# A hybrid decoder layer on one core: decode-state steps reordered, the second half of the up projection's operands put in another order, and the last quarter of the output finished like the other three

## Chip, cores and metric

The kernel runs on one core of one Trainium2 chip. The metric is the device time of one execution in microseconds (us). Each kernel is run several times and the median is given; the kernel before took 1743.32 us (three runs: 1743.06, 1743.32 and 1748.29).

## What is computed

One layer of a decoder, for a prompt of 1024 tokens and, beside it, 8 single new tokens of other sequences ("decode", with states given). All arrays are float32.

```python
D_MODEL, SEQ, DEC_BATCH, D_FF = 1024, 1024, 8, 2816
def decoder_layer(x, S_h, S_s, buf_s, buf_f, lb, w):
    h = rmsnorm(x, w['norm1_w'])
    q_r, f_r, i_r, g_r, z, xbc_r, dt_r = jnp.split(h @ w['w_in'], splits, axis=-1)
    ...
    o_a, S_h_new = hgrn2_mix(q, k, v, log_f, S_h)          # 8 heads, gated linear recurrence
    o_a = rmsnorm(o_a, w['hgrn_norm_w']) * silu(g_r)
    xbc, buf_s_new = causal_dwconv(xbc_r, buf_s, ...)
    ...
    y, S_s_new = ssd_scan(X * dt[..., None], A * dt, Bh, Ch, S_s)   # 16 heads, Mamba-2
    y = rmsnorm((y + D * X) * silu(z), w['ssm_norm_w'])
    x = x + concat([o_a, y]) @ w['w_out']
    h = rmsnorm(x, w['norm2_w'])
    gate, val = jnp.split(h @ w['w_up'], 2, axis=-1)       # 1024 -> 2 x 2816
    gate, buf_f_new = causal_dwconv(gate, buf_f, ...)      # width 3
    x = x + (silu(gate) * val) @ w['w_down']               # 2816 -> 1024
    return x, S_h_new, S_s_new, buf_s_new, buf_f_new
y = rmsnorm(x, final_norm_w)
```

The new states of both mixers and the last rows of both convolutions are outputs too. For a decode token the Mamba part is one step: the new state is `Sd = decay * Sd + B * x`, and its output is the sum over the state of `Sd * C`.

## The kernel before

**Precision.** Each large product runs as three TensorE (PE) products: both factors are split into a rounded part and a remainder (`hi` by a cast on ScalarE, ACT; `lo = x - hi` on VectorE, DVE), and high x high, high x low and low x high are summed. A group of products sums into one PSUM bank; some other engine then evicts the bank, and until it has done so no new group can start in that bank. There are three banks called `mm` for the big products (`ua` and `dn` below are such banks) and four called `mx` for all else (`ub`, `sT`, `st`, `yo`, `yd`, `fin`), and one `nx`.

**Stages**, by time in the profiled execution: input projection with both recurrences (to 805 us), output projection (to 1013), up projection (to 1466), down projection (to 1704), the final norm's blocks (to the end at 1741).

**What sets the order.** The order of the matmuls on PE is written out by hand: big products come as "jobs" that yield after every few matmuls, and small work is woven in between: `spread(x, n)` advances the generator `x` once in every n matmuls, `after(n, f)` calls `f` n matmuls later, `drive` and `finish` run jobs up to a named one. On the other engines and in the DMA queue (SP) a scheduler puts the instructions in an order from their data dependences and its own estimates; `tc.issue_after(i)` forbids it to place an instruction ahead of `i`. Each engine then works strictly in its order, so an instruction that waits holds up all that stand behind it there.

**The decode step of Mamba** (`ssm_decode`, lines 656 to 675) runs for 8 pairs of heads. For each and for four tokens at a time it loads `Bb` and `Cb` (B and C of the tokens, spread over the partitions) and `Sd` (the state); ACT multiplies `Sd` by the decay (line 669), DVE multiplies `Bb` by x (line 670) and adds it to `Sd` (671), GpSimd (POOL) multiplies by `Cb` (673), and DVE sums (674). This runs beside the last steps of the prompt's recurrence: `ssd_back` makes a chunk's output and the next state `S` (line 611), and `ssm_state_out` (633) transposes the final state on PE (bank `sT`, line 636), copies it on DVE to `so` (638) and stores it. The stage is called z here.

**The up projection.** For each of 22 column blocks j the product of a 2 x 2 block matrix of activations with a 2 x 2 block matrix of weights (gate and value columns) is made with seven products `p1` to `p7` in place of eight, Strassen's scheme in Winograd's form; it needs sums of blocks ahead of it and sums of products behind it. It is done for two rows of activation blocks, i = 0 (the first 516 tokens) and i = 1 (the other 516). `set_of(i)` prepares the seven operands: `comb` makes a sum `sm` (line 1352), `put` splits an operand into `uh` and `ul` (lines 1344 and 1345). `up_sums(j)` makes four sums of weights `wt` on POOL (line 1424); `up_split` splits these into `wh` and `wl` (1443, 1444). Of the products behind, `p7` adds on DVE (1478) and then has two subtractions on POOL (1479, 1480: `val` and `us`); `p2`, `p4` and `p3` add on DVE into `fext` (1486, 1494) and `val` (1506). For j = 0, row 0 comes whole before row 1 (order `FIRST`), and `set_of(1)` runs beside it. `set_norm(i, c)` makes the norm of a quarter of the tokens: one matmul into bank `n2ms` and three steps of DVE (lines 737 to 739, `nt`).

**The down projection** (`down`) sums 4 blocks of k at a time into a bank `dn` and adds it to x in DVE (line 1611). `act_load` splits its activations into `ah` and `al` (line 1154).

**The end.** The last two blocks of k are done by quarter of the tokens, in the order 3, 0, 1, 2. For quarters 3, 0 and 1: 48 `dn` matmuls, DVE adds them to x (line 1688), PE transposes x to rows of tokens (line 1695, bank `fin`), ACT squares and sums (1697), then a mean, a root, and the scaling: the first half of the columns in one DVE operation (1707), the second by an ACT copy (1704) and a POOL product; each half is stored. Quarter 2 is done in another way (`last_blocks`, lines 1655 to 1674): the product is made with tokens as rows at once, and x is added by multiplying it, split in two, with the identity on PE.

## Time and profile before

| | |
|---|---|
| median of three runs | 1743.32 us |
| the profiled execution's own time | 1742.79 us |
| its span, first to last instruction | 1741.1 us |
| PE, matmuls | 1705.4 us busy (98%) |
| PE, weight loads (beside the matmuls) | 1656.5 us (95%) |
| DVE | 1089.1 us (63%) |
| ACT | 789.8 us (45%) |
| POOL | 483.4 us (28%) |
| mean clock granted to PE | 0.997 of full speed |

The profiled execution is 1.7 us longer than its span, and half a microsecond under the median. "Busy" is the time in which at least one instruction of the engine ran; for PE the ends of matmuls are modelled. In rows of the timeline the first number is the start of an instruction in us from the start of the span, the second its duration; then engine, line of the code, operation, tile written `<-` tiles read, and in brackets the idle time of the engine just ahead of it with what ended this.

### The profile page before, as it was taken

What the parts mean: (1) busy time and instruction counts of PE and PEld (TensorE: products, weight loads), DVE (VectorE), ACT (ScalarE), POOL (GpSimd) and SP (SyncE); (2) the same over time, 40 slices, a digit from 0 to 9 for tenths busy, and PEclk for the clock granted to TensorE, in tenths of its full rate; (3) what the DMA queues carried; (4) which work ended last, traced back from release to release, by engine and by line L of the source; (5) the groups of instructions that cost most, each with busy time, mean ns of one, the idle gap of its engine ahead of it and who ended that gap; (6) DMA issues with size and microseconds to landing.
All of it is one profiled execution on the core that took longest, in us unless ns stands there. A gap on an engine that the chain in (4) does not pass through costs nothing. (4 is left out here: it accounts for less than half of the span.)

```text
span 1741.1 us, 38505 instructions
## 1 busy us (share of the span) xinstructions
PE 1705.4 (98%) x16111; PEld 1656.5 (95%) x16111; DVE 1089.1 (63%) x1983; ACT 789.8 (45%) x1441; POOL 483.4 (28%) x501
## 2 busy tenths in 40 slices
PE   7999999999999999999999989999999999999998
PEld 7999999999999999999999989999999999999997
DVE  6668666555565565567746777667676668544454
ACT  7677686344454354545334554333344334111124
POOL 2102131110120122011222266666666664000002
PEclk9999999999999999999999999999999999999999
DMA  5354334633434425335347712222222226322212
GB/s 165 73 123 120 96 91 144 186 103 105 130 94 120 115 88 142 118 99 178 119 145 252 230 53 87 97 74 74 74 80 80 97 75 240 138 90 77 86 44 98
DMA packets 250212, 200.22 MB, mean 115 GB/s; under 512 B 48020, under 2 KB 221574, under 8 KB 250022
## 3 DMA queue, kind: packets, MB, share of 16 engines
q1 hardware_dynamic: 249750, 197.67, 37.2%
q8 instruction: 126, 2.06, 0.5%
q14 instruction: 48, 0.39, 0.1%
q0 software_dynamic: 288, 0.10, 0.0%
HBM read 155.16 MB, written 46.95 MB: 116 GB/s over the span
## 5 line engine op out<-in xcount | busy, mean ns | idle before, releaser
L93 PE MATMUL mm<-hl,wh 128*128 128x344 f32 x1248 | 405.5, 325 | 0.0
L93 PE MATMUL mm<-hh,wh 128*128 128x344 f32 x1248 | 405.0, 325 | 0.0
L93 PE MATMUL mm<-hh,wl 128*128 128x344 f32 x1248 | 402.0, 322 | 0.0
L93 PEld LDWEIGHTS mm<-hl,wh 128*128 128x128 f32 x1248 | 235.4, 189 | 4.8 <-issue 4.2
L93 PEld LDWEIGHTS mm<-hh,wh 128*128 128x128 f32 x1248 | 235.4, 189 | 3.4 <-issue 2.8
L93 PEld LDWEIGHTS mm<-hh,wl 128*128 128x128 f32 x1248 | 235.6, 189 | 1.4 <-issue 1.2
L199 ACT CAST wh<-ws 128x1024 fp32r<-128x1024 f32 x96 | 100.6, 1048 | 238.8 <-PE dn L93 125.8
L93 PE MATMUL ub<-uh,wh 128*128 128x258 f32 x704 | 199.7, 284 | 4.1 <-DVE nt L737 3.3
L93 PE MATMUL ub<-uh,wl 128*128 128x258 f32 x704 | 198.9, 283 | 0.0
L93 PE MATMUL ub<-ul,wh 128*128 128x258 f32 x704 | 198.3, 282 | 0.0
L93 PE MATMUL dn<-ah,wh 128*128 128x256 f32 (+1 forms) x640 | 180.6, 282 | 1.1 <-DVE x L1611 1.1
L93 PE MATMUL dn<-al,wh 128*128 128x256 f32 (+1 forms) x640 | 180.2, 282 | 0.0
L93 PE MATMUL dn<-ah,wl 128*128 128x256 f32 (+1 forms) x640 | 179.7, 281 | 0.0
L201 DVE TENSOR_TENSOR wl<-ws,wh 128x1024 fp32r<-128x1024 f32 x88 | 115.3, 1310 | 81.0 <-ACT wh L199 81.0
L93 PE MATMUL ua<-uh,wh 128*128 128x258 f32 x528 | 149.6, 283 | 2.6 <-DVE val L1506 1.3
L93 PE MATMUL mm<-mh,wh 128*128 128x258 f32 x512 | 146.3, 286 | 4.9 <-DVE x L1233 4.1
L93 PE MATMUL ua<-uh,wl 128*128 128x258 f32 x528 | 149.3, 283 | 0.1
L93 PE MATMUL ua<-ul,wh 128*128 128x258 f32 x528 | 148.7, 282 | 0.0
L93 PE MATMUL mm<-ml,wh 128*128 128x258 f32 x512 | 145.1, 283 | 0.0
L93 PE MATMUL mm<-mh,wl 128*128 128x258 f32 x512 | 144.7, 283 | 0.0
L93 PEld LDWEIGHTS ub<-uh,wh 128*128 128x128 f32 x704 | 133.0, 189 | 4.5 <-DVE nt L737 3.5
L1444 DVE TENSOR_TENSOR wl<-wt,wh 128x512 fp32r<-128x512 f32 x88 | 89.6, 1037 | 75.1 <-ACT wh L1443 75.0
(394 smaller groups left out, 3982.5 us busy)
## 6 DMA issues: line engine op xcount, KB each, us to landing
ws<-in_w_in_dram SPq DMA_DIRECT2D x52, 512.0 KB
ws<-in_w_up_dram SPq DMA_DIRECT2D x44, 512.0 KB
ws<-in_w_out_dram SPq DMA_DIRECT2D x24, 512.0 KB
act_d<-val SPq DMA_DIRECT2D x22, 516.0 KB
al<-act_d SPq DMA_DIRECT2D x22, 516.0 KB
ws<-in_w_down_dram SPq DMA_DIRECT2D x22, 512.0 KB
ml<-mix_d SPq DMA_DIRECT2D x48, 172.0 KB
csb<-cs_d SPq DMA_DIRECT2D x32, 256.0 KB
```

The lines of the kernel that those rows point to most:

```text
L93: PE.matmul(out, lhsT, rhs, start=start, stop=stop)
L199: A.copy(wh[:, :n], ws[:, :n])
L201: V.tensor_tensor(wl[:, :n], ws[:, :n], wh[:, :n].bitcast(F32), op=ALU.subtract)
L1444: V.tensor_tensor(lo[:, cs], sums[name], hi[:, cs].bitcast(F32), op=ALU.subtract)
```

## The change

It has four parts in the code; elsewhere the two kernels are the same.

```diff
@@ ssm_state_out, ssm_decode, head_in @@
+    freed = [None, None]
     def ssm_state_out(g):
...
-        V.tensor_copy(so, ps)
+        freed[0] = V.tensor_copy(so, ps)
...
             for b in range(4):
-                A.activation(d4(Sd)[:, b, :], d4(Sd)[:, b, :], AF.Copy, scale=ddb[:, 1, j, b0 + b:b0 + b + 1])
-            V.tensor_tensor(d4(Bb), d4(Bb), cb(xdd[:, 0, bs]), op=ALU.mult)
+                with tc.issue_after(freed[1].ins):
+                    A.activation(d4(Sd)[:, b, :], d4(Sd)[:, b, :], AF.Copy, scale=ddb[:, 1, j, b0 + b:b0 + b + 1])
+            with tc.issue_after(freed[0].ins):
+                V.tensor_tensor(d4(Bb), d4(Bb), cb(xdd[:, 0, bs]), op=ALU.mult)
...
-                A.activation(t[n][:, cs], ps, func, scale=0.5 if n == "f" else 1.0)
+                freed[1] = A.activation(t[n][:, cs], ps, func, scale=0.5 if n == "f" else 1.0)
@@ set_of(1) @@
             yield from put("p2", a2, "big")
-            yield from put("p4", b2, "big")
             yield from comb(s_, V, b1, b2, ALU.subtract)
             yield from comb(s_, V, two(s_[0]), a1, ALU.subtract)
             yield from comb(s_, G, two(s_[1]), a2, ALU.add)
             up_sums(1, combed[0])
+            yield from put("p4", b2, "big")
             yield from put("p6", [s_[1]], "hT")
@@ ups, and the call of set_norm for row 1 @@
-            if n == (2 if j else 5) and j + 1 < FT:
+            if n == (2 if j else 4) and j + 1 < FT:
                 up_load(j + 1)
-        after(93, lambda: (set_norm(1, 0), set_norm(1, 1)))
+        after(130, lambda: (set_norm(1, 0), set_norm(1, 1)))
@@ the end @@
-    def halved():
...
-    def summed(b):
...
-    def last_blocks():
...
     for c in (3, 0, 1, 2):
         cs = quarters[c]
-        if c == 2:
-            for _ in split_:
-                pass
-            last_blocks()
-            break
-        if c == 0:
-            split_ = halved()
-            spread(split_, 3)
         for m in range(KT):
...
-                if i:
+                if i and c != 2:
                     A.activation(ot[i][:n], tb[i][:n, :], AF.Copy, scale=ss[:n, 3:4])
                     G.tensor_tensor(ot[i][:n], ot[i][:n], fw[:n, ds], op=ALU.mult)
                 else:
```

In the changed kernel a line stands 2 lines lower from `ssm_state_out` on and 4 lower from the `Bb` product on, so that line 670 is its line 674 and line 1611 its line 1615. Three places show how the instructions now stand.

**DVE in stage z**, at the end of the prompt's recurrence. `Bb` is the product of `ssm_decode`, `S` the last state that `ssm_state_out` transposes, `ecs` and `xbc` the chunk's output. Before:

```order
L670 TENSOR_TENSOR Bb_3479<-Bb_3479,xdd_3477 128x512
L605 TENSOR_TENSOR ecs_3336<-yo_3339,ecs_3336 128x512
L670 TENSOR_TENSOR Bb_3494<-Bb_3494,xdd_3477 128x512
L611 TENSOR_TENSOR S_3347<-S_3347,st_3345 128x512
L621 TENSOR_TENSOR ecs_3336<-yd_3350,ecs_3336 128x512
L671 TENSOR_TENSOR Sd_3483<-Sd_3483,Bb_3479 128x512
```

And now:

```order
L605 TENSOR_TENSOR ecs_3336<-yo_3339,ecs_3336 128x512
L611 TENSOR_TENSOR S_3347<-S_3347,st_3345 128x512
L621 TENSOR_TENSOR ecs_3336<-yd_3350,ecs_3336 128x512
L624 SCALAR_TENSOR_TENSOR xbc_1678<-xbc_1678,d_bc,ecs_3336 128x128
L624 SCALAR_TENSOR_TENSOR xbc_1864<-xbc_1864,d_bc,ecs_3336 128x128
L624 SCALAR_TENSOR_TENSOR xbc_2047<-xbc_2047,d_bc,ecs_3336 128x128
L624 SCALAR_TENSOR_TENSOR xbc_2230<-xbc_2230,d_bc,ecs_3336 128x128
L640 COPY so_3382<-sT_3377 128x512
L201 TENSOR_TENSOR wl_3387<-ws_3385,wh_3386 128x1024
L674 TENSOR_TENSOR Bb_3479<-Bb_3479,xdd_3477 128x512
L674 TENSOR_TENSOR Bb_3494<-Bb_3494,xdd_3477 128x512
```

The two `Bb` products, which stood ahead of the add that finishes `S`, now stand behind the copy of the transposed state.

**POOL in the up projection**, from the last sum for the norm (`n2r`) to the products of row 1: `val_12299` and `us` are the two subtractions behind row 0's `p7`, `sm` the combination for row 1's `p3`, `wt` the weight sums of j = 1. Before:

```order
L1251 TENSOR_TENSOR n2r_812<-n2r_812,n2sq_12285 128x258
L1479 TENSOR_TENSOR val_12299<-us_12398,us_12416 128x258
L1480 TENSOR_TENSOR us_12380<-us_12398,us_12380 128x258
L1352 TENSOR_TENSOR sm_12430<-sm_12405,x_1170_10444 128x516
L1352 TENSOR_TENSOR sm_12430<-sm_12405,x_1187_10581 128x516
L1424 TENSOR_TENSOR wt_12447<-ws_12423 128x512
L1424 TENSOR_TENSOR wt_12449<-wt_12447,ws_12421 128x512
L1424 TENSOR_TENSOR wt_12451<-ws_12421,ws_12423 128x512
L1424 TENSOR_TENSOR wt_12453<-wt_12449,ws_12421 128x512
```

And now:

```order
L1356 TENSOR_TENSOR sm_12406<-sm_12384,x_1170_10444 128x516
L1255 TENSOR_TENSOR n2r_812<-n2r_812,n2sq_12285 128x258
L1356 TENSOR_TENSOR sm_12406<-sm_12384,x_1187_10581 128x516
L1428 TENSOR_TENSOR wt_12427<-ws_12399 128x512
L1428 TENSOR_TENSOR wt_12429<-wt_12427,ws_12397 128x512
L1428 TENSOR_TENSOR wt_12431<-ws_12397,ws_12399 128x512
L1428 TENSOR_TENSOR wt_12433<-wt_12429,ws_12397 128x512
L1483 TENSOR_TENSOR val_12299<-us_12395,us_12417 128x258
L1484 TENSOR_TENSOR us_12377<-us_12395,us_12377 128x258
```

Both `sm` halves and all four `wt` have moved ahead of the two subtractions. On DVE the three steps of the norm of row 1, which stood ahead of the addition of row 1's `p2` into `fext`, stand behind it now.

**DVE at the start of the down projection**, where the last block of the up projection (`val` times `fext`, line 1525) and the first banks `dn` meet. Before:

```order
L1154 TENSOR_TENSOR al_18067<-al_18067,ah_18066 128x1032
L1611 TENSOR_TENSOR x_2296_18092<-x_2296_18092,dn_18094 128x256
L1525 TENSOR_TENSOR val_17817<-val_17817,fext_17816 128x1032
L1611 TENSOR_TENSOR x_2296_18092<-x_2296_18092,dn_18108 128x256
L1154 TENSOR_TENSOR al_18072<-al_18072,ah_18071 128x1032
L1611 TENSOR_TENSOR x_2296_18092<-x_2296_18092,dn_18122 128x256
```

And now:

```order
L1158 TENSOR_TENSOR al_18067<-al_18067,ah_18066 128x1032
L1615 TENSOR_TENSOR x_2296_18092<-x_2296_18092,dn_18094 128x256
L1529 TENSOR_TENSOR val_17817<-val_17817,fext_17816 128x1032
L1158 TENSOR_TENSOR al_18072<-al_18072,ah_18071 128x1032
L1615 TENSOR_TENSOR x_2296_18092<-x_2296_18092,dn_18108 128x256
L1615 TENSOR_TENSOR x_2296_18092<-x_2296_18092,dn_18122 128x256
```

The second addition, of bank `dn_18108`, has moved behind the split `al_18072`; the diff does not touch these lines, the scheduler chose so.

More of the change, by code (lines that the diff above doesn't have):

```diff
@@ L1624, in hybrid_layer @@
         wd.append((hi, lo))
-    halves_ = []
-    def halved():
-        identr = tl("us", "idr", F32R)[:, :P]
-        A.copy(identr, ident)
-        halves_.append(identr)
-        for h4 in range(2):
-            hi, lo = tl("x5", "xfh", F32R)[:, :1024], tl("x5", "xfl", F32R)[:, :1024]
-            halves_.append((hi, lo))
-            for m in range(4):
-                x_, at_ = xT[4 * h4 + m][:, quarters[2]], slice(m * 256, (m + 1) * 256)
-                A.copy(hi[:, at_], x_)
-                V.tensor_tensor(lo[:, at_], x_, hi[:, at_].bitcast(F32), op=ALU.subtract)
-                yield
@@ L1640, in summed @@
-    def summed(b):
-        t0 = quarters[2].start + b * P
-        tb = [bank("fin"), bank("fin")]
-        for i in range(2):
-            ds, first_ = slice(i * 512, (i + 1) * 512), True
-            for k in range(nk):
-                for a, x in ((0, 0), (1, 0), (0, 1)):
-                    mm(tb[i], acts[k][a][:, t0:t0 + P], wd[k][x][:, ds], start=first_, stop=k == nk - 1 and x == 1)
-                    tick()
-                    if first_:
-                        first_ = False
-                        for m in range(4):
-                            for x_ in halves_[1 + i]:
-                                mm(tb[i][:, blk[m]], x_[:, m * 256 + b * P:m * 256 + (b + 1) * P], halves_[0],
-                                   start=False, stop=False)
-        return t0, tb
@@ L1657, in last_blocks @@
-    def last_blocks():
-        for b in range(2):
-            t0, tb = summed(b)
-            ss = keep.tile([P, 4], F32, tag="ss", bufs=4, name=nm("fss"))
-            ot, sq = ([tl("t", "ot") for _ in range(2)] for _ in range(2))
-            for i in range(2):
-                ds = slice(i * 512, (i + 1) * 512)
-                A.activation(sq[i], tb[i], AF.Square, accum_out=ss[:, i:i + 1])
-                V.tensor_tensor(ot[i], tb[i], fw[:, ds], op=ALU.mult)
-            V.tensor_tensor(ss[:, 2:3], ss[:, 0:1], ss[:, 1:2], op=ALU.add)
-            A.activation(ss[:, 3:4], ss[:, 2:3], AF.Sqrt, bias=epsc, scale=1.0 / DM)
-            V.reciprocal(ss[:, 3:4], ss[:, 3:4])
-            for i in range(2):
-                if i:
-                    A.activation(ot[i], ot[i], AF.Copy, scale=ss[:, 3:4])
-                else:
-                    V.tensor_scalar(ot[i], ot[i], ss[:, 3:4], None, op0=ALU.mult)
-                SP.dma_start(y_prompt[0, t0:t0 + P, i * 512:(i + 1) * 512], ot[i])
@@ L1702, in hybrid_layer @@
                 ds = slice(i * 512, (i + 1) * 512)
-                if i:
+                if i and c != 2:
                     A.activation(ot[i][:n], tb[i][:n, :], AF.Copy, scale=ss[:n, 3:4])
```

## Prediction

> **What bounds the kernel now.** PE is busy for 98% of the span (the table ahead), so a change is worth what it takes from PE's waits, from matmuls, from a slow clock, or from the stretch behind the last matmul. I read PE's waits first. The view of its waits from 300 us on groups them by what PE waited for; the numbers are us in all, times, us at most:

> ```profile
> PE mm L93 <- DVE x L1233: 4.1, 6, 0.9
> PE ub L93 <- DVE nt L737: 3.3, 1, 3.3
> PE sT L636 <- DVE S L611: 2.4, 1, 2.4
> PE fin L93 <- ACT ot L1704: 1.7, 1, 1.7
> PE ua L93 <- DVE val L1506: 1.3, 1, 1.3
> PE dn L93 <- DVE x L1611: 1.1, 1, 1.1
> PE ua L93 <- DVE us L1478: 1.0, 1, 1.0
> PE ub L93 <- ACT us L1474: 0.8, 1, 0.8
> ```

> The first row is six short waits of the output projection, which the change leaves alone. Each of the others is one single wait at a place that the change touches: `sT` in stage z, four in the up projection, `dn` at the start of the down projection, `fin` at the end. So I take the four places one by one.

> **Stage z.** DVE's timeline around the 2.4, and PE's windows there (length, PE busy with its matmuls, granted clock, DMA share, GB/s):

> ```profile
> 311.18 0.70 DVE L670 TENSOR_TENSOR Bb<-Bb,xdd 128x512 f32<-128x512 f32 x1 [2.07 <-DMA Bb<-bc_d]
> 311.79 0.69 DVE L605 TENSOR_TENSOR ecs<-yo,ecs 128x512 f32<-128x512 f32 x1
> 313.39 0.69 DVE L670 TENSOR_TENSOR Bb<-Bb,xdd 128x512 f32<-128x512 f32 x1 [0.92 <-DMA Bb<-bc_d]
> 314.00 0.68 DVE L611 TENSOR_TENSOR S<-S,st 128x512 f32<-128x512 f32 x1
> ```
> ```profile
> 312.10:315.50 3.40, 0.96 (x8) 1.00 0.61 205
> 315.50:318.90 3.40, 3.40 (x14) 0.50 0.28 77
> 318.90:322.30 3.40, 3.40 (x24) 1.00 0.45 109
> ```

> `S` ends at 314.68 because both `Bb` products ahead of it wait for loads. With them moved behind, DVE goes from 309.11 (311.18 less 2.07) straight to `ecs` and `S`: 309.11 + 0.69 + 0.68 gives about 310.5. PE wants `S` at about 312.3 (2.44 us ahead of its restart near 314.7), so the wait of 2.4 goes, with nothing late in its place on DVE. After the wait PE ran one window at half clock, 14 matmuls where the next window has 24: ten matmuls of 3.40 / 24 = 0.142 us, or 1.4, and with its edges I take 1.6. So z gives **−4.0**; at the worst, if the clock falls in spite of it, −2.4.

> [...] The rows speak for the cause all the same: the window ahead of the slow one holds only 0.96 us of matmuls, and the waits of 0.8 to 1.3 left no slow window.

> What moves later is the decode step itself: ACT's scalings of `Sd` now stand behind head 0's last eviction, some 8 us later, and the loads of `Sd` follow. I cost that at nothing: PE does not read its results until heads later, and ACT is idle for more than half of this stage. If a scaling waits for its load, though, evictions of PE's banks stand behind it; that is the rival below, and its rows (a timeline row of ACT, and a row on what the 24 scalings waited for in all: us, times):

> ```profile
> 312.71 1.28 ACT L669 ACTIVATE Sd<-Sd,ddb 128x128 f32<-128x128 f32 x4 [6.80 <-DMA Sd<-in_state_ssm_dram]
> ```
> ```profile
>   DMA Sd<-in_state_ssm_dram: 11.1, 4
> ```

> The first wait, 6.8, is for the first load, which now has 8 us more; the other three share 4.3. Three banks of 24 matmuls are 10.2 us; with one of them being filled, 6.8 remain as cover, less 1.28 for the four scalings: 5.5. No later wait seen reaches that.

> **Up projection.** POOL, then DVE, then PE around the 3.3:

> ```profile
> 1026.07 1.61 POOL L1479 TENSOR_TENSOR val<-us,us 128x258 f32<-128x258 f32 x1 [7.55 <-issue]
> 1027.65 0.74 POOL L1480 TENSOR_TENSOR us<-us,us 128x258 f32<-128x258 f32 x1
> 1028.34 2.36 POOL L1352 TENSOR_TENSOR sm<-sm,x 128x516 f32<-128x516 f32 x2
> 1030.66 1.26 POOL L1424 TENSOR_TENSOR wt<-ws 128x512 f32<-128x512 f32 x1
> ```
> ```profile
> 1021.08 0.69 DVE L1352 TENSOR_TENSOR sm<-sm,x 128x516 f32<-128x516 f32 x1
> ...
> 1031.82 1.23 DVE L1345 TENSOR_TENSOR ul<-sm,uh 128x1032 fp32r<-128x1032 f32 x1 [2.98 <-ACT uh L1344]
> 1032.97 0.75 DVE L737 SCALAR_TENSOR_TENSOR nt<-n2ms,n2r 128x258 f32<-128x258 f32 x2
> ```
> ```profile
> 1033.78 0.39 PE L93 MATMUL ub<-uh,wh 128*128 128x258 f32 x1 [3.27 <-DVE nt L737]
> ```

> Before, POOL idles for 7.55 us, then does `val`, `us` and, late, `sm`; the last split on DVE waits for that `sm`, the norm's `nt` stands behind the split, and PE gets its bank at 1033.78 instead of 1030.5 (3.27 earlier). Now POOL does both `sm` as soon as DVE has made their input (1021.8), then the four `wt`, and only then `val` and `us`, while DVE's addition of row 0's `p3` needs that `us` and everything behind it waits: a split of 1.23, then the eviction (0.41 by its width) that frees the bank.

> POOL's chain: 2.36 + 4 x 1.26 + 2 x 0.74 = 8.9, from 1021.8 to 1030.7. That is the lower bound, if nothing disturbs it. The upper one: an operation of POOL beside one of DVE takes longer (1.61 against 0.74 for the same shape, while DVE did a split), as if one waited for the other. In this time DVE has two splits of 516 columns at about 0.7 and three of 1032 at 1.23, 5.1 in all; if all of that comes on top, POOL ends at 1035.8. Behind it DVE needs 0.41 + 1.23 + 0.41 = 2.05. So PE's bank comes at 1032.7 to 1037.8. I take the middle, 1035.3, since some splits wait for casts on ACT and will not all fall beside POOL: 1.5 **later** than now, not earlier.

> [...]

> What follows is given back by the later waits. A row of the chain of waits gives PE's pace, and the first instruction behind the last of these waits:

> ```profile
> 1065.63 5.77 PE ub L93 x48
> ```

> Twelve matmuls are one product: 5.77 / 4 = 1.44. From 1033.78 to 1065.63 lie 19 products, 27.4, and 4.45 of waits: 3.1 in the rows (0.8, 1.0, 1.3) and 1.35 of restarts. The 1.0 waits for an addition into `us` and the 0.8 for a copy by ACT, both held up by the late `sm` and `wt`; with these early, both go with their restarts. The third waits for an addition into `val` behind weights of j = 2, whose load is issued one product earlier; I leave it at 1.3 with 0.4 for its restart. So 1035.3 + 27.4 + 1.7 = 1064.4 instead of 1065.63: **−1.2**. At 1032.7 it would be −3.8; at 1037.8 the third wait is covered (PE comes later to it), and 1037.8 + 27.4 is 1065.2, −0.4, or +1.2 if a window at half clock follows the long wait. That the 3.3 brought none shows here, PE busy for 1.60 at full clock:

> ```profile
> 1028.90:1032.30 3.40, 1.60 (x14) 1.00 0.00 0
> ```

> **Start of the down projection.**

> ```profile
> 1472.03 0.41 DVE L1611 TENSOR_TENSOR x<-x,dn 128x256 f32<-128x256 f32 x1
> 1472.36 1.22 DVE L1154 TENSOR_TENSOR al<-al,ah 128x1032 fp32r<-128x1032 f32 x1
> ```
> ```profile
> 1472.57 0.31 PE L93 MATMUL dn<-ah,wh 128*128 128x256 f32 x1
> ```

> PE starts its next group at 1472.57, as soon as the addition of 1472.03 has freed the bank. Now the split of 1.22 comes first: the bank is free 1.2 later, PE waits that long, and nothing behind gives it back, since PE has no other wait to the end. **+1.15**; at best 0, if PE's three banks cover it.

> **The end.** Rows of the chain of waits, a square on ACT, a scaling on DVE, and PE's window:

> ```profile
> 1716.01 4.13 PE dn L93 x35
> 1720.14 1.14 PE fin L1695 x9
> ...
> 1723.83 11.02 PE fin L93 x56
> ...
> 1736.97 0.72 ACT ot L1671
> ```
> ```profile
> 1718.66 0.60 ACT L1697 ACTIVATE ot<-fin 128x512 f32<-128x512 f32 x1 [1.59 <-DMA out_dram<-ot]
> ```
> ```profile
> 1725.83 0.75 DVE L1707 SCALAR_TENSOR_TENSOR ot<-fin,fss,fw 128x512 f32<-128x512 f32 x1
> ```
> ```profile
> 1725.20:1728.60 3.40, 3.40 (x12) 0.50 0.49 181
> ```

> Before, quarter 2 needs `fin` banks at once, and PE waits 1.7 for them, to 1723.83. Then come its products with the identity matmuls, half clock in one window, to 1734.85. Behind PE stand a square, a mean, a root and a scaling, to 1737.69; the span ends 3.4 later, with the last store.

> Now quarter 2 begins with `dn` matmuls in the `mm` banks, so PE goes on at about 1722.1 (1723.83 less 1.7). 48 at 4.13 / 35 = 0.118 are 5.7: 1727.8. Last addition 0.41 and a handover: 1728.3. Sixteen transposes at 1.14 / 9 = 0.127: most of block 0's stand ahead of the last x, so block 0 is ready at 1728.7 and block 1 at 1729.6. Four squares of 0.7 (0.60 and its readout) from 1728.4 on, with a halt of about 0.3 for a buffer that a store still holds: 1731.5. DVE is at block 0's two scalings of 0.75 until 1732.6; then mean, root and reciprocal (0.5 with handovers) and two scalings: 1734.6. With the same 3.4 the span ends at 1738.0 instead of 1741.1: **−3.1**. The bounds: a buffer as late as in the row of 1718.66 costs 1.6 (−1.5); block 1's mean ahead of block 0's scalings on DVE gains 1.4 (−4.5). No half clock is left there, since PE has no wait.

> **Sum.** −4.0 − 1.2 + 1.15 − 3.1 = −7.15. The profiled execution took 1742.79, so it would be 1735.6; the median of the runs shown is half a microsecond higher, so 1736.1.

> **The rivals.**
> *The cover holds and nothing is shared on POOL and DVE:* up −3.8, down 0, the end −4.5, z −4.0: −12.3, 1731. Against it speaks the 1.61.
> *Waits change places:* the slow window in z stays (−2.4), up −0.4 + 1.6 by a slow window, the end −1.5, down +1.15: −1.55, 1741.7; with one of these alone, up to 1739. For it: POOL is loaded ahead of DVE's critical addition. Against: the waits of up were short of a slow window even at 3.3.
> *Slower:* ACT's queue in z. If a load of `Sd` starts only when the store of the half step before has landed, a scaling waits a round trip, twice 6.8 = 13.6, and each such wait costs PE 13.6 less 5.5, 8.1. Of the six half steps two such make +16.2: 1752. It decides from waits of over 5.5 on. Against it: the other three waits sum to 4.3.

> **How the numbers follow.** The forecast 0.60, the larger gain 0.12, waits that change places 0.22, the slower case 0.06. About 0.3%, 5.2 us, is what a measurement of this kernel can tell from no change; faster by more means below 1738.1. The forecast (but for 0.02 of it) and the larger gain lie there: 0.70; waits that change places and that rest: 0.24; slower: 0.06. The range, 1730.5 to 1742, takes in the bounds of up, down and end, and the smaller gain; the slower case stays out.

> **What would show it.** Right: `S` ends near 310.5, no wait at `sT`, clock 1.00 from 315 to 322; PE's wait ahead of the `ub` product at 1030 grows to some 5 and the 1.0 and 0.8 are gone; a new wait of about 1.2 at the third or fourth `dn`; no wait ahead of the last quarter, and some 8.4 us from the last matmul to the end. Wrong: waits of ACT for `Sd` of over 5.5 with PE idle behind them, or a window at clock 0.50 in the up projection.

## The result, and the profile after

The changed kernel took 1738.82 us (median of ten runs, 1736.43 to 1743.80), the kernel before 1744.29 in ten runs beside it: a ratio of 0.9966, 95% interval 0.9954 to 0.9978, or 5.5 to 6 us less. The forecast was 1736.1, with a range to 1742.

The profiled execution of the changed kernel is its slowest run (span 1742.1 us), so it must be read by stage, not by its end. The view of PE's waits from 300 us on (us in all, times, us at most):

```profile
PE mm L93 <- DVE x L1237: 5.0, 7, 1.7
PE n2ms L93 <- DVE fext L1498: 3.0, 1, 3.0
PE mm L93 <- issue: 2.3, 1, 2.3
PE dn L93 <- DVE x L1615: 2.3, 2, 1.4
PE ub L93 <- DVE fext L1490: 1.9, 1, 1.9
PE mm L93 <- ACT sg L930: 1.7, 1, 1.7
```

`sT`, the three short waits of the up projection (`us` twice, `val`) and `fin` are gone. In the up projection stand two waits, 3.0 and 1.9, where one of 3.3 stood; `dn` has two instead of one. The three `mm` rows lie at the last input projection and in the output projection, outside the four places of the change; they vary from run to run (below).

**Stage z**, DVE's timeline:

```profile
310.29 0.68 DVE L605 TENSOR_TENSOR ecs<-yo,ecs 128x512 f32<-128x512 f32 x1
310.88 0.67 DVE L611 TENSOR_TENSOR S<-S,st 128x512 f32<-128x512 f32 x1
```

No `Bb` stands between: `S` ends at 311.55 instead of 314.68, in an execution that was already 0.9 late, and PE does not wait. And ACT's scalings of `Sd` wait for a load once in 24, for 2.7 us instead of 11.1 in all:

```profile
326.53 2.44 ACT L672 ACTIVATE Sd<-Sd,ddb 128x128 f32<-128x128 f32 x8
...
352.67 0.40 ACT L672 ACTIVATE Sd<-Sd,ddb 128x128 f32<-128x128 f32 x1 [2.74 <-DMA Sd<-in_state_ssm_dram]
```

PE does not wait for ACT anywhere between 305 and 375 us.

**Up projection**, POOL, then DVE (pieces of it), then PE's windows behind the second wait (length, PE busy, granted clock, DMA share, GB/s):

```profile
1025.94 1.75 POOL L1428 TENSOR_TENSOR wt<-ws 128x512 f32<-128x512 f32 x1
1027.77 1.64 POOL L1428 TENSOR_TENSOR wt<-wt,ws 128x512 f32<-128x512 f32 x1
1029.36 2.28 POOL L1428 TENSOR_TENSOR wt<-ws,ws 128x512 f32<-128x512 f32 x1
1031.60 2.26 POOL L1428 TENSOR_TENSOR wt<-wt,ws 128x512 f32<-128x512 f32 x1
1033.82 1.72 POOL L1483 TENSOR_TENSOR val<-us,us 128x258 f32<-128x258 f32 x1
1035.50 0.73 POOL L1484 TENSOR_TENSOR us<-us,us 128x258 f32<-128x258 f32 x1
```
```profile
1028.17 4.57 DVE L1349 TENSOR_TENSOR ul<-sm,uh 128x1032 fp32r<-128x1032 f32 x2
...
1034.88 0.41 DVE L1498 TENSOR_TENSOR fext<-us,ub 128x258 f32<-128x258 f32 x1
1036.27 0.42 DVE L1510 TENSOR_TENSOR val<-us,ua 128x258 f32<-128x258 f32 x1 [0.98 <-POOL us L1484]
...
1037.76 0.42 DVE L1490 TENSOR_TENSOR fext<-us,ub 128x258 f32<-128x258 f32 x1
```
```profile
1035.83:1039.24 3.41, 1.53 (x8) 0.73 0.00 0
1039.24:1042.65 3.41, 3.41 (x17) 0.50 0.00 0
1042.65:1046.07 3.42, 3.42 (x25) 0.77 0.00 0
```

PE's first wait ends with the eviction at 1034.88, which stands behind a row of splits on DVE; DVE was not idle ahead of it. The second ends with the eviction at 1037.76: the subtractions come last on POOL, DVE waits 0.98 for `us`, and a split stands between. Beside each other both engines were slow here. `wt` took 1.64 to 2.28, against 1.26 (1030.66 before) where DVE was idle, and the two splits took 4.57, against 2.38 in the code before, where POOL was idle:

```profile
1023.23 2.38 DVE L1345 TENSOR_TENSOR ul<-sm,uh 128x1032 fp32r<-128x1032 f32 x2
```

Then PE runs at half clock for 6.8 us.

**Start of the down projection**, DVE:

```profile
1474.25 0.41 DVE L1615 TENSOR_TENSOR x<-x,dn 128x256 f32<-128x256 f32 x1
1474.58 1.22 DVE L1529 TENSOR_TENSOR val<-val,fext 128x1032 f32<-128x1032 f32 x1
1475.73 1.22 DVE L1158 TENSOR_TENSOR al<-al,ah 128x1032 fp32r<-128x1032 f32 x1
1476.87 1.08 DVE L1615 TENSOR_TENSOR x<-x,dn 128x256 f32<-128x256 f32 x3
```

Three additions of `x` run in a row at 1476.87: their banks had been full while the split ran.

**The end**, chain of waits:

```profile
1729.02 3.80 PE dn L93 x30
1732.83 0.45 PE fin L1640 x4
```

PE goes through to the end of its last transposes at 1734.57, and the span ends 7.5 later.

Since one execution is a draw, the table sets stages of all profiled executions side by side, each from the start of PE's first matmul of one kind to that of the next: z from the first `sT` (of the first of two states, near 202 us) to the first `vd` (a transpose of the first decode step of the next stage), up from the first `ua` to the first `dn`, down from there to the first `fin`, and the end from there to the end of the span. In brackets, for up, for how many us the clock was at half behind its waits.

| execution | z | up | down | end |
|---|---|---|---|---|
| before | 171.5 | 452.0 (0) | 237.7 | 37.9 |
| changed, first | 167.7 | 452.3 (6.8) | 239.6 | 34.1 |
| changed, second | 167.2 | 450.9 (3.4) | 239.3 | 34.0 |
| z alone | 168.6 | 452.1 (6.8) | 237.7 | 36.3 |
| up alone | 169.8 | 451.6 (6.8) | 237.7 | 36.2 |
| end alone | 171.5 | 452.0 (3.4) | 238.8 | 34.0 |
| roots alone | 173.3 | 450.3 (3.4) | 237.7 | 37.5 |
| p4 alone | 170.7 | 452.7 (6.8) | 237.9 | 36.2 |
| weights behind | 169.0 | 449.9 (0) | 238.8 | 34.0 |
| splits behind | 167.2 | 452.0 (6.8) | 236.3 | 34.1 |
| ACT and POOL scale | 168.0 | 450.8 (6.8) | 239.2 | 34.4 |
| three repairs, first | 169.4 | 449.0 (0) | 236.3 | 34.3 |
| three repairs, second | 167.9 | 449.2 (3.4) | 236.4 | 34.2 |
| roots, end, z, splits | 167.6 | 450.3 (3.4) | 237.1 | 33.8 |

### The profile page after: what moved, and what is told of

The parts are those of the page before. It is cut to its first block, busy times and chain, and to the rows that moved or that the text cites. A ratio compares the mean times of both kernels' runs of the same rounds, so it can differ in the third digit from the quotient of the medians.

```text
span 1742.1 us, 38520 instructions
## 1 busy us (share of the span) xinstructions
PE 1704.6 (98%) x16119; PEld 1657.3 (95%) x16119; DVE 1092.0 (63%) x1981; ACT 784.7 (45%) x1430; POOL 486.1 (28%) x501
## 5 line engine op out<-in xcount | busy, mean ns | idle before, releaser
L93 PE MATMUL mm<-hl,wh 128*128 128x344 f32 x1248 | 405.1, 325 | 0.0
L93 PE MATMUL mm<-hh,wh 128*128 128x344 f32 x1248 | 404.5, 325 | 0.0
L93 PE MATMUL mm<-hh,wl 128*128 128x344 f32 x1248 | 401.6, 322 | 0.0
L93 PEld LDWEIGHTS mm<-hl,wh 128*128 128x128 f32 x1248 | 235.0, 188 | 4.8 <-issue 4.2
L93 PEld LDWEIGHTS mm<-hh,wh 128*128 128x128 f32 x1248 | 235.0, 188 | 4.0 <-issue 3.4
L93 PEld LDWEIGHTS mm<-hh,wl 128*128 128x128 f32 x1248 | 235.2, 188 | 1.4 <-issue 1.2
L93 PE MATMUL ub<-uh,wh 128*128 128x258 f32 x704 | 200.2, 284 | 1.9 <-DVE fext L1490 1.9
L93 PE MATMUL ub<-uh,wl 128*128 128x258 f32 x704 | 199.5, 283 | 0.0
L93 PE MATMUL ub<-ul,wh 128*128 128x258 f32 x704 | 199.1, 283 | 0.0
L93 PE MATMUL dn<-ah,wh 128*128 128x256 f32 (+1 forms) x640 | 180.7, 282 | 2.3 <-DVE x L1615 2.3
L93 PE MATMUL dn<-al,wh 128*128 128x256 f32 (+1 forms) x640 | 180.2, 282 | 0.0
L93 PE MATMUL dn<-ah,wl 128*128 128x256 f32 (+1 forms) x640 | 179.8, 281 | 0.2 <-DVE wl L201 0.2
L93 PE MATMUL mm<-mh,wh 128*128 128x258 f32 x512 | 146.7, 286 | 9.1 <-DVE x L1237 5.0
L93 PE MATMUL ua<-uh,wh 128*128 128x258 f32 x528 | 149.9, 284 | 0.0
L93 PE MATMUL ua<-uh,wl 128*128 128x258 f32 x528 | 149.8, 284 | 0.0
L93 PE MATMUL ua<-ul,wh 128*128 128x258 f32 x528 | 149.4, 283 | 0.0
L93 PE MATMUL mm<-ml,wh 128*128 128x258 f32 x512 | 145.4, 284 | 0.0
L93 PE MATMUL mm<-mh,wl 128*128 128x258 f32 x512 | 145.0, 283 | 0.0
L93 PEld LDWEIGHTS ub<-uh,wh 128*128 128x128 f32 x704 | 133.5, 190 | 2.1 <-DVE fext L1490 2.1
L93 PEld LDWEIGHTS ub<-ul,wh 128*128 128x128 f32 x704 | 134.2, 191 | 0.0
```

The source lines that it names most:

```text
L93: PE.matmul(out, lhsT, rhs, start=start, stop=stop)
```

## The experiments

**One part at a time, on the kernel before.** z alone has the `freed` edits; up alone has the three edits of the up projection; end alone has the last quarter's. The diffs are those pieces of the change's diff, without the rest. The changed kernel ran beside them once more.

> The kernel before with the z part alone (Bb behind the state's copy, Sd scalings behind head 0's last eviction). Theory 'each place by itself': S ends near 310.5 to 311.5 us, no wait of PE at sT, no window at half clock near 315, and from the transposes of the states on everything stands 3.8 to 4.0 us earlier: 4 us less than the kernel before. Rival 'paid back later': the decode step that now runs later holds up ACT's evictions or POOL, and half or more of the 4 us is lost again between 330 and 1013 us (the changed kernel's one profile lost 0.6 at 380, 1.8 at 803 and 3 between 819 and 1013): 0 to 2 us less in all.

> The kernel before with the up projection's part alone. Theory 'POOL serial': both waits of the changed kernel come (PE waits some 3.0 for fext of row 0's p4, then some 1.9 for fext of row 1's p2, a window at half clock follows, the waits of 1.0, 0.8 and 1.3 are gone); from the first product of the up projection to the first of the down projection 452.0 to 452.5 us, against 452.0 before: no gain, 0 to +0.5. Rival 'my sum': no slow window, and the stage 1.2 us shorter. The start of the down projection keeps the order of before, with one wait of about 1.1 there.

> The kernel before with the last quarter done like the other three, and nothing else. Theory: the end gains (first fin transpose to end of span 34.1 instead of 37.9, -3.8), and the scheduler's changed order at the start of the down projection (the second addition of x behind a split) costs 1.2 to 1.9 there: 2 to 2.6 us less in all. The order of DVE shows that this edit alone brings that change of order. Rival: the start of the down projection is slower because of the up part (its last block ends in another state), and the tail alone gains the whole 3.8.

> The changed kernel once more, for a second profile. Theory 'each place by itself': z -3.9, up +0.3, start of the down projection +1.9, the end -3.8, -5.5 in all, and the loss of some 5 us between 378 and 1013 us of the first profile does not come again (no wait of PE of 2.3 at 819, of 1.7 at 803). Rival 'paid back later': the loss comes again in this profile, so it belongs to the change.

Measured, as ratios to the kernel before: z 0.9976 (0.9967 to 0.9985), about -4.2 us; up 0.9998 (0.9988 to 1.0009), nothing that shows, though the interval reaches to -2.1 us; end 0.9981 (0.9972 to 0.9990), about -3.3; the changed kernel again 0.9966 (0.9954 to 0.9978), -5.9. The three parts add up to -7.8; the whole has less, within the intervals. z is not paid back later. From the first `sT` to the first `ua`, PE took 809.0 us on average over the nine executions with that edit (the table's, and those below) and 812.4 over the five without. The first profile of the changed kernel lost 3 us in the output projection; the second took 206.3 us there against 208.0 before, and none of the seven others took over 209.0, so that loss is not the change's.

The slower start of the down projection is the end's doing: end alone has it (238.8 against 237.7), up alone has not. An edit of the last stage made the scheduler place an addition behind a split 250 us earlier. The rival for that part is refuted.

**Which edit of the up projection does what.** Two more on the kernel before:

```diff
# roots alone
-        after(93, lambda: (set_norm(1, 0), set_norm(1, 1)))
+        after(130, lambda: (set_norm(1, 0), set_norm(1, 1)))
# p4 alone
-            yield from put("p4", b2, "big")
             yield from comb(s_, V, b1, b2, ALU.subtract)
...
             up_sums(1, combed[0])
+            yield from put("p4", b2, "big")
```

> The kernel before with the roots of row 1 alone moved (130 matmuls instead of 93). POOL's order stays that of before (subtractions first, then the late sum sm, then the weights). Theory 'the late sm is the first wait': DVE's last split of row 1 still ends near 18.5 us after the first product of the up projection... 19.6 (1033.05 less 1013.49 before), and the bank is freed by the addition of row 1's p2 right behind it, so PE's first wait stays at 2.8 to 3.3 us; the 0.8 to 1.3 us waits behind it stay too, and the stage takes 452.0 again. Rival: the three steps of the norm ahead of that addition were the wait, and without them it falls by 0.7 or more and the stage with it.

> The kernel before with the p4 operand's move alone (the combinations and weight sums ahead of it), roots at 93 matmuls and the load as before. The order of POOL is then that of the changed kernel. Theory 'POOL serial': this one edit makes the long wait: PE waits 4.5 to 5.5 us in one piece for the bank that the roots hold or that p2's addition frees, and the waits of 1.0, 0.8 and 1.3 go, as in the changed kernel; stage 450.5 to 452.5 depending on slow windows. Rival: without the later roots the wait is split otherwise and the late waits stay: stage over 453.

Each of the two has one execution. PE's waits in the up projection with the roots alone:

```profile
PE ub L93 <- DVE fext L1486: 3.1, 1, 3.1
PE dn L93 <- DVE x L1611: 1.1, 1, 1.1
PE ua L93 <- DVE val L1506: 1.0, 1, 1.0
```

And with p4 alone:

```profile
PE ub L93 <- DVE fext L1494: 3.7, 1, 3.7
PE ub L93 <- DVE nt L737: 1.2, 1, 1.2
```

p4's move alone makes the long wait, 4.9, though in two pieces and not in one, and the stage takes 452.7, just above what was expected. The roots' move leaves the first wait at 3.1 (expected), but two of the short waits go and the stage falls to 450.3, which neither theory had. The first wait is set by the late split, with the norm's steps behind it or without; what those steps held up is what follows. DVE's addition of row 1's p2 starts 19.5 us after the stage's first product (1037.92 less 1018.45) instead of 24.1 (1037.60 less 1013.49), and the weights' splits behind it follow.

**Repairs of the changed kernel.** Weights behind: the four weight sums are put behind the subtractions again, by naming the second one (`sub`, kept in `combed[1]`) as the instruction that they may not pass.

```diff
-            up_sums(1, combed[0])
             yield from put("p4", b2, "big")
+            up_sums(1, combed[1])
```

Splits behind: the second round's `act_load` calls are written behind the first column block's sums (`r0 == 0`).

```diff
-            nxt = [act_load(r0 + RND + k) for k in range(min(RND, FT - r0 - RND))]
+            nxt = []
+            if r0:
+                nxt = [act_load(r0 + RND + k) for k in range(min(RND, FT - r0 - RND))]
...
+                    if not r0 and not nxt:
+                        nxt = [act_load(RND + k) for k in range(RND)]
```

ACT and POOL scale: `if i and c != 2:` becomes `if i:`. Three repairs: the first two of these, and `if i and (c != 2 or t0 == cs.start):`, so that the last quarter's first block scales its second half on ACT and POOL.

> The changed kernel, with the four weight sums of j = 1 on POOL put behind the two subtractions of row 0's p7 again (the sums sm stay early). Theory 'POOL serial': the 4.9 us of waits in the up projection's second row came from the four wt ahead of the subtractions; now val and us run some 7 us earlier, DVE's addition of row 0's p3 and what stands behind it follow, and both waits together fall to under 1.5 us, with no slow window. The gain is then some 3.5 us less what the later wt bring (waits of PE of up to 2 us for weights of j = 1 or sums behind them). Stage from the first product of the up projection to the first of the down projection 449 to 450.5 us instead of 450.9 to 452.4. Rival 'DVE bound': DVE's splits and POOL's sums still exclude each other; the waits only change their names and sum to 4 to 5 us again.

> The changed kernel, with the loads and splits of the second round of activations of the down projection written behind the first column block's sums (before: ahead of them). DVE then has two additions of x ahead of the split, as it had one before. Theory: both waits at the start of the down projection (1.1 to 1.4 and 0.9) go or fall to under 0.5 in all, and the stage from the first dn to the first fin falls from 239.3 to about 237.3. Rival: the wait is for the last block of the up projection, whose steps stand in the same place on DVE, and only the 0.9 goes: 238.2.

> The changed kernel, with the second half of the last quarter's columns scaled by ACT's copy and POOL's product as in the other quarters (before: DVE scales both). Theory 'the gain is on PE': the stretch from the last matmul to the end of the span stays within 0.5 of 7.5 us, and the kernel keeps the gain of the tail. Rival 'the gain is in the scaling': the stretch grows by over 1 us.

> The changed kernel with three repairs: weight sums behind the subtractions, second round's splits behind the first sums, and of the last quarter's two blocks only the last scaled by DVE alone (the first leaves its second half to ACT and POOL, so the last block's mean comes earlier). Theory: -2 for the first, -2 for the second, -0.5 for the third: some 4 us less than the changed kernel, near 1734.5. Rival: what PE gains in the up projection is lost to a later wait of the same chain, as in the kernel before, and only the start of the down projection gains: 1736.5.

Weights behind: 0.9951 (0.9936 to 0.9966). Its waits:

```profile
PE ub L93 <- DVE fext L1492: 1.9, 1, 1.9
PE ua L93 <- DVE val L1512: 1.6, 1, 1.6
PE ua L93 <- DVE us L1482: 1.4, 1, 1.4
```

Here both theories are half right. The two waits of 4.9 in all became one of 1.9, and PE restarts behind it 18.9 us after the stage's first product (1030.25 less 1011.39) instead of 22.15, so the four `wt` ahead of the subtractions were the cause: the subtractions come earlier, and the splits ahead of them run at their old pace (2.36 and 1.22 instead of 4.57 and 1.96). But two others came back, and the sum is 4.9 again. The stage still takes 449.9, the shortest till then, and its clock stayed whole: three waits of under 2 us cost less than two of 3.0 and 1.9 with half clock behind them. That is one execution; which part of the gain is the clock's, it does not tell.

Splits behind: 0.9951 (0.9936 to 0.9965), down 236.3 instead of 239.3, no wait at `dn`. DVE has both additions ahead of the split now:

```profile
1466.20 0.75 DVE L1617 TENSOR_TENSOR x<-x,dn 128x256 f32<-128x256 f32 x2
1466.86 1.68 DVE L1158 TENSOR_TENSOR al<-al,ah 128x1032 fp32r<-128x1032 f32 x1
```

That takes away even the wait of 1.1 that the kernel before had; the rival said that only the 0.9 would go.

ACT and POOL scale: 0.9969 (0.9956 to 0.9981), and from the last matmul to the end 7.7 us against 7.5. Which engine scaled made no more difference than that; the end's gain is on PE. Three repairs: 0.9931 (0.9914 to 0.9947), 1733.64 us. Its third repair brought nothing: DVE finished 0.7 us sooner after PE's last matmul (3.9 against 4.5), and the span ended as long after it as without (7.6 against 7.5). Three stores of 256 KB come at once there; that they are the limit was not tried.

**Roots, end, z and splits, without p4's move**, beside the three repairs again:

> The changed kernel with the p4 operand's move and the earlier load taken back (roots at 130 matmuls, z and the end as changed) and the repair at the start of the down projection. Theory 'the roots' move is the gain, p4's move a loss': waits of PE in the up projection of 3.1 and 1.0 in all (as with the roots alone), stage 449 to 450.3 us, and 0.5 to 2 us less than the changed kernel with the same repair of the down projection (1736.2). Rival 'PE-bound either way': the stage is 451 to 452, as with p4 moved.

> The version with the three repairs once more, for a second profile on the same chip as the run before it: waits in the up projection of 1.4 to 1.9 each (three of them), no window at half clock behind them, stage 449 to 450 us; time some 10 us under the kernel before. Rival: the first profile was lucky, and slow windows come here too, with the stage at 450.7 or more.

0.9933 (0.9920 to 0.9946) and 0.9936 (0.9919 to 0.9953): equal, some 11 us under the kernel before, and both under the changed kernel's 0.9966. The first has the waits (3.1 and 1.0) and the stage that were expected, but gains some 3 us on the changed kernel with the repair of the down projection (0.9951), more than the 0.5 to 2 expected. The second profile of the three repairs did have a slow window behind the wait of 1.9, so the first was lucky as its rival said; yet the stage took 449.2, because the wait of 1.4 went meanwhile:

```profile
PE ub L93 <- DVE fext L1492: 1.9, 1, 1.9
PE ua L93 <- DVE val L1512: 1.0, 1, 1.0
```

With p4 not moved, and one slow window too, it took 450.3. So p4's move is worth about 1 us if the weights stay behind the subtractions, in one profile each; the times do not tell the two apart.

## Why the prediction was right, step by step

In all four places what was forecast to move moved, and the waits that were forecast to go went; its sum was -7.15, and -5.5 to -6 was measured. By its own signs it failed in one place: a window at half clock in the up projection was to show it wrong there.

**z, -4.0: right.** z alone gave -4.2, and the wait of 2.4 is gone in each profile with the edit. `S` ends at 311.55, which is 310.6 when the 0.9 by which that execution was late is taken off; the forecast had 310.5. Over all executions the stage has 168.1 with it (nine) and 171.4 without (five). The half clock that the forecast counted at 1.6 was there in three of the five without the edit, so that term is an average of about 1, not a fixed price. The rival of ACT's queue needed waits for `Sd` of over 5.5: the longest in any profile with the edit is 3.1, and PE waits for ACT nowhere near it. (Its six half steps are those of `ssm_decode`, which runs for three of the eight pairs of heads; the other five go another way, `decode_beside`.)

**Up, -1.2: right in its chain, wrong in what follows.** The forecast put PE's restart at 1035.3, 21.8 us after the stage's first product; it came 22.15 after it (1038.23 less 1016.08), and by the chain that was named: `us` on POOL, the addition into `val`, a split, the eviction. That the middle of the bounds came so near is partly luck. Half of the late `sm` ran early, at 1020.68, so POOL's chain from the other half on is 7.7 us alone (1.18 + 5.04 + 1.48) and not 8.9; but it took 11.4 (1024.79 to 1036.23): 3.7 of the 5.1 of splits came on top, not half of them, and all five splits fell beside POOL's chain. What the splits lose was not counted: they took 9.9 us (3.35 + 4.57 + 1.96) instead of the 4.9 before, which gave PE its wait of 3.0 for row 0's `p4`; since the second wait ends later, the restart did not suffer by it. Of what follows, "I leave it at 1.3" failed: the third wait went as well. In its place came what the forecast had only as a rival, half clock behind the long wait, in each of the five profiles with the order of the changed kernel, for one window of 3.4 us or two. Their stage is 451.5 on average against 452.0: -0.5.

**Start of the down projection, +1.15: right where it stands alone.** End alone has +1.1, in a wait of 0.9 and its restart. Together with the up part it is 1.5 to 1.9, and 1.1 again with the weights behind: the first `dn` wait grows, or the stage begins a little sooner than DVE can serve it; which of the two was not settled.

**The end, -3.1: right, and its size depends on the draw.** Against the profiled execution before it is -3.8, against the average of its five executions (36.8) -2.8. The forecast took the half clock of that one execution for a fixed part; it was there in two of five. The stretch behind the last matmul was forecast at 8.4 and is 7.5.

Summed over the averages: -3.3 - 0.5 + 1.6 - 2.8 = -5.0. So what the forecast missed are one term, the slow windows on the wrong side in up, and that windows at half clock in one profile were counted whole in z and at the end. Half a microsecond to one, by which the measured times fell further than these stages, is not placed.

## What to carry to other kernels

In z the wait of 2.4 that was taken away was worth about its length even where no slow clock followed it (169.8 and 170.7, against 168.1 without it), but the slow clock only as often as it came: look at more than one profile before counting it. When sums are moved forward on a busy engine, look at what now stands behind them and what runs beside them: with the weights' sums moved back and the rest of the edit left, the up projection took 449.0 to 449.9, against 451.5 with the whole edit and 452.0 with none of it. And compare the order on every engine after an edit, also in stages that it does not touch: here an edit of the last 20 us cost 1 us in a stage 250 us ahead, and a repair there of a few lines brought 3 us, more than the two waits in it (2.0 to 2.3).

## What the runs showed of the hardware

The same wait, in the same code, was followed by half clock in one execution and not in another. In stage z with the wait of 2.4, up alone, then end alone:

```profile
312.30:315.70 3.40, 0.99 (x8) 1.00 0.66 221
315.70:319.10 3.40, 3.40 (x24) 1.00 0.29 77
```
```profile
311.10:314.50 3.40, 1.08 (x7) 1.00 0.87 285
314.50:317.90 3.40, 3.37 (x14) 0.53 0.27 77
```

```profile
311.29:314.70 3.41, 1.06 (x8) 1.00 0.80 264
```
```profile
310.48:313.89 3.41, 2.41 (x19) 1.00 1.06 353
313.89:317.31 3.42, 2.00 (x14) 1.00 0.16 42
```

The next window ran at half clock in the first and at full clock in the second. All 14 executions were read in windows of 0.5 us from 300 to 335 us, 795 to 835, 1015 to 1060, 1460 to 1490, and from 1700 to PE's last matmul. Put together by that step they give some 630 windows at full clock: each of the 15 in which PE was busy for 1.51 us or less was followed by half clock, and none with 1.76 or more; between these, from 1.56 to 1.73, both came.

With the order of the kernel before, the slow windows cost the up projection no time: it took 452.0 us with none (before), 452.0 with one (end alone) and 452.1 with two (z alone). Behind the 3.3 there were three short waits of 3.1 in all, two of 2.1 and one of 1.2, since PE, being later, no longer met the others.
